# Chunk kernels of a state-space scan as products of the input tables with the output matrix

## Chip, cores and metric

The kernel runs on one core of a Trainium2 chip. The metric is the time of one execution in device microseconds (us); less is better. Before the change three runs took 1483.23, 1479.48 and 1482.27 us, a median of 1482.27.

## What is computed

Two transformer-like blocks over 528 positions (512 tokens and 16 meta tokens) of width 1024. The change concerns the first mixer of the first block, which has two branches: a state-space branch (S5, 32 groups of 16 channels with 64 complex states) and four mLSTM heads. Cut to the state-space branch, the reference is:

```python
dt = jnp.exp(log_dt)[:, None]
mag = jnp.exp(lam_re * dt)
ab_re, ab_im = mag * jnp.cos(lam_im * dt), mag * jnp.sin(lam_im * dt)   # a = exp(lambda dt)
bb = z * b                                                              # complex, z = (a - 1) / lambda
x[t] = a * x[t - 1] + bb @ u[t]                                         # associative scan over 528 positions
y = real(c @ x) + d * u
y_a = gelu(y); y_a = y_a * sigmoid(y_a @ w_glu)
```

Everything is float32. Large products are made of three passes (high by high, high by low, low by high part).

## The kernel before

The front of the program (`mixer`, from line 261) makes everything from eight input tiles. The 528 positions are cut into 66 chunks of 8. For each group the branch needs four things: what each chunk adds to the state (`inputs`), the recurrence from chunk to chunk (`recur`), what the state adds to the outputs of the next chunk (`back`, with the output table `CA`), and what the inputs of a chunk do to the outputs of the same chunk (`intra`, a Toeplitz matrix of the chunk kernel). The 32 groups go through in four sets of 8, m = 0 to 3.

- `prep(m)` (line 729) makes the input table `wt` on VectorE (`table`, lines 718 to 720: three operations over the whole table), turns it by eight transposes on TensorE (line 740), and ScalarE copies it to `ws` (line 742). `inputs(m)` multiplies `ws` with the chunk inputs `U` (line 752); ScalarE copies the result to `X` (line 756) and issues two transfers that put the swapped halves beside it (line 758).
- `recur` (line 800) is the recurrence on GpSimd: 64 steps of three operations each (lines 805 to 807), every step on all 32 groups, so that it starts after the last `X` transfer. Its result is read by the products of `X` with `CA` in `back` (line 821), which TensorE meets during the third head.
- `kernel(m)` (line 765) makes the output table `CA` (lines 718 to 720 again, now with 9 powers), multiplies `BB1` with it (line 776, eight products), copies the result to `kt` (line 778), adds the direct term `dm` (line 782), writes `kt` to a scratch buffer `kd` in DRAM behind 112 zeros (SyncE issues it, line 784), and reads it back through an overlapping pattern as the Toeplitz tile `tm` (ScalarE issues it, line 786). `intra(m)` multiplies `tm` with `U` (line 796).
- `Mlstm.proj(h)` makes the four projections of head h (q, k, v, output gate); each is 48 products (line 178) of a weight tile that `split_w` loads (SyncE, line 165) and splits into `wh` (ScalarE, line 167) and `wl` (VectorE, line 168).

Products of the branch share four PSUM buffers, `m`, with the attention core of the heads; the projections have two buffers, `d`. A list scheduler fixes the order on every engine when the program is built; `issue_after` and the order of calls steer it. Each engine runs its own list in order, and a transfer that ScalarE or SyncE issues stands in that list too: what comes behind it waits while it waits.

In time: the four input projections (u0 to u3) come first, then head 0 with `prep` and `inputs` between its projections, then head 1 with `kernel` and `intra` between them, then the cores of heads 0 to 3 beside the projections of heads 2 and 3 and the output side.

Of the kernel before, what the change touches and what calls it, by code (L numbers as in the profile page):

```python
# [9 lines left out]
F = mybir.dt.float32  # L10
# [12 lines left out]
G, NP, GH, NCH = 32, 64, 16, 66  # L23
# [237 lines left out]
def mixer(c):  # L261
    nc, tc, I = c.nc, c.tc, c.I
    V, A, P = nc.vector, nc.scalar, nc.gpsimd
    xh, xl = c.xh, c.xl
    with ExitStack() as ctx:
# [8 lines left out]
        def dense_ps():  # L274
            return pd.tile([128, 2, 512], F, name="d", tag="d")
# [8 lines left out]
        ssm = Ssm(c, hp, fs, misc, dr)  # L284
# [33 lines left out]
        def proj_full(idx, w=None):  # L318
            w = w or c.split_w(I["w1"][idx], 1024)
            ps = dense_ps()  # L320
            c.mm3([ps[:, 0, :264], ps[:, 1, :264]], w, 8,
                  lambda k, p: xh[:, k, 264 * p : 264 * p + 264], lambda k, p: xl[:, k, 264 * p : 264 * p + 264])
            return ps
# [16 lines left out]
        ml.gates()  # L340
        ssm.load()
        coeffs, first, root = ssm.coeffs(), ml.proj(0), c.root
        for m in range(4):
            with tc.high_priority():
                w = c.split_w(I["w1"][m], 1024) if m else w0
            ps = proj_full(m, w)
            u = fs2.tile([128, 8, NCH], F, name="u", tag="sa", bufs=2)
            for p in range(2):
                V.tensor_tensor(u[:, ::-1, 33 * p : 33 * p + 33].rearrange("p j c -> p c j"),
                                ps[:, p, :264].rearrange("p (c j) -> p c j", j=8),  # L350
                                rstd[:, 264 * p : 264 * p + 264].rearrange("p (c j) -> p c j", j=8), op=OP.mult)
            ssm.load_u(m, u)
            with tc.issue_after(root.ins) if m else ExitStack():
                if m < 2:
                    next(coeffs, None)
        for m in range(4):
            next(first, None)
            ssm.prep(m)
            if m:
                ssm.inputs(m - 1)  # L360
        ssm.inputs(3)
        ssm.recur()
        ssm.powers()
        ssm.pads()
        first = ml.proj(1)
        ssm.kernel(0)
        ssm.kernel(1)
        ml.rows(fs2)
        for m in range(4):
            next(first, None)  # L370
            dense = c.mm
            with tc.issue_after(ml.last.ins):
                if m < 2:
                    ssm.kernel(m + 2)
            with tc.issue_after(dense.ins):
                if m:
                    ssm.intra(m - 1)
                if m == 3:
                    ssm.intra(3)
        for _ in first:  # L380
            pass
        fctx.close()
# [79 lines left out]
        for m in range(8):  # L462
            w = c.split_w(I["wo1"][m], 1024)
            ps = dense_ps()
# [6 lines left out]
        for m in range(8):  # L471
# [3 lines left out]
            t = op.tile([128, 2, HF], F, name="pt", tag="pt", bufs=2)  # L475
# [104 lines left out]
class Ssm:  # L580


    def __init__(self, c, pool, front, misc, dram):
# [8 lines left out]
        self.AR = pool.tile([128, 2, 2, G], F, name="AR")  # L592
        self.U, self.ws, self.tm = {}, {}, {}

# [18 lines left out]
    def coeffs(self):  # L613
        c, nc, ss = self.c, self.c.nc, self.ss
        V, A = nc.vector, nc.scalar
        lr, li, sg = c.v("lam_re", 0, G), c.v("lam_im", 0, G), c.v("sgn")
        t = self.t32
        dt = c.exp_small(c.v("log_dt", 0, G), G)
        a = t("a")
# [14 lines left out]
        q = t("q")  # L634
# [25 lines left out]
        nr, den, zr, zi, m = t("nr"), t("den"), t("zr"), t("zi"), t("m")  # L660
# [20 lines left out]
        def bc(x):  # L681
            return x.unsqueeze(2).to_broadcast([128, G, GH])

        V.tensor_mul(self.BB1, B1, bc(zr))
        V.tensor_mul(m3, B2, bc(zis))
        V.tensor_sub(self.BB1, self.BB1, m3)
# [12 lines left out]

    def powers(self):  # L700
        V = self.c.nc.vector
        t = self.fs2.tile([128, 2, 9, G], F, name="cpow", tag="ws", bufs=2)
        self.prs, self.pin = t[:, 0], t[:, 1]
        for o, x, a in ((self.prs, self.pr, self.c.v("sgn")), (self.pin, self.pi, -1.0)):
            V.tensor_scalar_mul(o.rearrange("p e g -> p (e g)"), x.rearrange("p e g -> p (e g)"), a)

    def table(self, eng, out, tmp, x1, x2, p1, p2, gs, e0, ne):

# [13 lines left out]
    def load_u(self, m, u):  # L722
        nc = self.c.nc
        U = self.U[m] = self.hp.tile([128, 8, NCH], F, name="U", tag="qkv", bufs=11)
        ud = self.dr.tile([8, 128, NCH], F, name="ud", tag="ud")
        nc.scalar.dma_start(ud.rearrange("r p c -> p r c"), u)
        nc.scalar.dma_start(U.rearrange("p g c -> p (g c)"), ud.rearrange("r (h g) c -> (r h) (g c)", g=8))

    def prep(self, m):
        c, nc, ss, misc = self.c, self.c.nc, self.ss, self.misc  # L730
        V, A = nc.vector, nc.scalar
        gs = 8 * m
        wt = ss.tile([128, 8, 8, GH], F, name="wt", tag="t4", bufs=2)
        tmp = ss.tile([128, 8, 8, GH], F, name="tmp", tag="tt", bufs=1)
        self.table(V, wt, tmp, self.BB1, self.BB2, self.pr, self.pis, gs, 0, 8)
        ws = self.fs2.tile([128, 8, 128], F, name="ws", tag="ws", bufs=2)
        for q in range(2):
            ps = misc()
            for j in range(4):
                nc.tensor.transpose(ps[:, 128 * j : 128 * j + 128],  # L740
                                    wt[:, 4 * q + j].rearrange("p e h -> p (e h)"), c.idn)
            A.copy(ws[:, 4 * q : 4 * q + 4].rearrange("p g m -> p (g m)"), ps)
        self.ws[m] = ws

    def inputs(self, m):
        c, nc, misc = self.c, self.c.nc, self.misc
        A = nc.scalar
        gs, U, ws = 8 * m, self.U[m], self.ws[m]
        for q in range(2):
            ps = misc()  # L750
            for j in range(4):
                nc.tensor.matmul(ps[:, NCH * j : NCH * j + NCH], ws[:, 4 * q + j], U[:, 4 * q + j],
                                 start=True, stop=True)
# [5 lines left out]

    def ctable(self, m):  # L760
        tmp = self.ss.tile([128, 8, 9, GH], F, name="tmp", tag="t4", bufs=2)
        self.table(self.c.nc.vector, self.CA[:, 8 * m : 8 * m + 8], tmp, self.rc[:, 0], self.rc[:, 1], self.prs, self.pin,
                   8 * m, 0, 9)

    def kernel(self, m):
        c, nc, ss, misc = self.c, self.c.nc, self.ss, self.misc
        V, A, P = nc.vector, nc.scalar, nc.gpsimd
        gs = 8 * m
        U = self.U[m]
        ca = self.CA[:, gs : gs + 8]  # L770
        self.ctable(m)
        kt = self.fs2.tile([GH, 8, 128], F, name="kt", tag="kt", bufs=1)
        for q in range(2):
            ps = misc()
            for j in range(4):
                nc.tensor.matmul(ps[:GH, 128 * j : 128 * j + 128], self.BB1[:, gs + 4 * q + j],
                                 ca[:, 4 * q + j, 0:8].rearrange("p e h -> p (e h)"), start=True, stop=True)
            A.copy(kt[:, 4 * q : 4 * q + 4].rearrange("p g x -> p (g x)"), ps[:GH])
        dm = self.fs2.tile([GH, 8, GH], F, name="dm")
        V.tensor_mul(dm, c.idn[:GH, :GH].unsqueeze(1).to_broadcast([GH, 8, GH]),  # L780
                     c.v("d_t", gs, 8, GH).unsqueeze(2).to_broadcast([GH, 8, GH]))
        V.tensor_add(kt[:, :, :GH], kt[:, :, :GH], dm)
        kd = self.kd[m]
        nc.sync.dma_start(kd[:, :, 112:], kt)
        tm = self.tm[m] = self.fs2.tile([128, 8, 128], F, name="tm", tag="tm", bufs=3)
        nc.scalar.dma_start(tm, bass.AP(tensor=kd.tensor, offset=kd.offset,
                                        ap=[[16, 8], [1920, GH], [240, 8], [1, 128]]))

    def intra(self, m):

        nc, misc, A = self.c.nc, self.misc, self.c.nc.scalar
        gs, U, tm = 8 * m, self.U[m], self.tm.pop(m)
        for q in range(2):
# [790 lines left out]
@with_exitstack  # L1584
def build(ctx, tc, I, O, dbg=False, stages=3):
    c = Core(tc, ctx, I, O, dbg)
    with ExitStack() as c.fctx:
        c.pd = c.fctx.enter_context(tc.tile_pool(name="pd", bufs=2, space=PSUM))
        c.pm = c.fctx.enter_context(tc.tile_pool(name="pm", bufs=4, space=PSUM))
        rr = mixer(c)  # L1590
        if stages == 1:
            return
        ffn(c, rr)
        c.wpx = None
    if stages == 2:
        return
    with tc.tile_pool(name="apd", bufs=3, space=PSUM) as c.pd, tc.tile_pool(name="apo", bufs=1, space=PSUM) as c.po:
        attn(c)
        mlp(c)
# [15 lines left out]
```

## Time and profile before

| | |
|---|---|
| runs, median | 1482.27 us |
| profiled execution, its own time | 1480.72 us |
| its span (first to last instruction) | 1478.7 us |
| TensorE (PE) busy | 1436.9 us, 97% |
| VectorE (DVE) busy | 821.3 us, 56% |
| ScalarE (ACT) busy | 644.9 us, 44% |
| GpSimd (POOL) busy | 310.8 us, 21% |
| granted clock of TensorE, mean | 0.991 |

The span is cut by the profile into 40 equal slices; the digit of TensorE's granted clock is 9 (full speed) in all but the fourth, from 111 to 148 us, where it is 7. A row of the timeline gives the start and the length in us, engine, line, operation, what it writes and reads, how many, and in brackets how long the engine had been idle before and what ended that.

### The profile page before, as it was taken

What the parts mean: (1) busy time and instruction counts of PE and PEld (TensorE: products, weight loads), DVE (VectorE), ACT (ScalarE), POOL (GpSimd) and SP (SyncE); (2) the same over time, 40 slices, a digit from 0 to 9 for tenths busy, and PEclk for the clock granted to TensorE, in tenths of its full rate; (3) what the DMA queues carried; (4) which work ended last, traced back from release to release, by engine and by line L of the source; (5) the groups of instructions that cost most, each with busy time, mean ns of one, the idle gap of its engine ahead of it and who ended that gap; (6) DMA issues with size and microseconds to landing.
All of it is one profiled execution on the core that took longest, in us unless ns stands there. A gap on an engine that the chain in (4) does not pass through costs nothing.

```text
span 1478.7 us, 22651 instructions
## 1 busy us (share of the span) xinstructions
PE 1436.9 (97%) x9050; PEld 1295.2 (88%) x9050; DVE 821.3 (56%) x1463; ACT 644.9 (44%) x1032; POOL 310.8 (21%) x383
## 2 busy tenths in 40 slices
PE   7997999999999999999999899999998999999998
PEld 7996999999998998889988799999786788888887
DVE  8792654654437653256643668788776542244321
ACT  4453666733334433233332457677654531134310
POOL 0048860010124210001111513223444000000000
PEclk9997999999999999999999999999999999999999
DMA  5534123232522322332222133333222322322330
GB/s 171 145 90 89 58 71 89 66 107 81 175 90 71 100 85 85 109 107 87 79 88 92 44 116 114 110 99 101 67 73 93 104 100 100 100 90 96 107 121 29
DMA packets 62341, 140.33 MB, mean 95 GB/s; under 512 B 14742, under 2 KB 26902, under 8 KB 62236
## 3 DMA queue, kind: packets, MB, share of 16 engines
q1 hardware_dynamic: 44416, 126.72, 26.8%
q10 hardware_dynamic: 17820, 12.17, 3.6%
q8 instruction: 71, 1.16, 0.3%
q14 instruction: 34, 0.28, 0.1%
HBM read 128.83 MB, written 4.76 MB: 90 GB/s over the span
## 4 chain that ended last, share of the span: by engine, by line
PE 85%; DVE 7%; DMA 3%; issue 2%; ACT 1%; POOL 1%; ACTq 0%; DVEq 0%; POOLq 0%
PE d L178 17%; PE fm L178 16%; PE mp L178 12%; PE ad L178 9%; PE ad L1193 8%; PE fg L178 8%; PE ad L1404 3%; PE ao L178 3%; PE at L1314 1%; DMA kd<-kt 1%; DMA ud<-u 1%; PE m L999 1%; PE as L1289 1%; PE m L986 1%; PE as L1285 1%
## 5 line engine op out<-in xcount | busy, mean ns | idle before, releaser
L167 ACT CAST wh<-wr 128x1024 fp32r<-128x1024 f32 (+2 forms) x240 | 232.9, 972 | 534.0 <-PE fm L178 101.1
L168 DVE TENSOR_TENSOR wl<-wr,wh 128x1024 fp32r<-128x1024 f32 (+2 forms) x240 | 294.0, 1227 | 210.8 <-ACT wh L167 208.9
L178 PE MATMUL d<-xh,wl 128*128 128x258 f32 (+1 forms) x576 | 121.0, 290 | 1.7 <-DVE wl L168 1.7
L178 PE MATMUL d<-xh,wh 128*128 128x258 f32 (+1 forms) x576 | 121.3, 292 | 0.0
L178 PE MATMUL d<-xl,wh 128*128 128x258 f32 (+1 forms) x576 | 120.1, 289 | 0.0
L1193 PE MATMUL ad<-wh,xh 128*128 128x256 f32 x384 | 111.2, 293 | 2.5 <-ACT wh L167 1.3
L1193 PE MATMUL ad<-wh,xl 128*128 128x256 f32 x384 | 110.4, 289 | 1.4 <-DVE xl L570 1.2
L1193 PE MATMUL ad<-wl,xh 128*128 128x256 f32 x384 | 110.1, 289 | 0.5 <-DVE wl L168 0.4
L178 PEld LDWEIGHTS d<-xh,wl 128*128 128x128 f32 x576 | 91.4, 193 | 4.6 <-issue 2.3
L178 PEld LDWEIGHTS d<-xh,wh 128*128 128x128 f32 x576 | 91.4, 193 | 2.5 <-issue 1.0
L178 PEld LDWEIGHTS d<-xl,wh 128*128 128x128 f32 x576 | 91.7, 193 | 0.6 <-issue 0.4
L1116 POOL TENSOR_TENSOR gt<-gt,ga 128x512 f32<-128x512 f32 x22 | 31.5, 1434 | 267.5 <-ACT wh L167 202.9
L1193 PEld LDWEIGHTS ad<-wh,xh 128*128 128x128 f32 x384 | 74.0, 194 | 3.7 <-ACT xh L569 1.6
L1193 PEld LDWEIGHTS ad<-wh,xl 128*128 128x128 f32 x384 | 74.4, 194 | 2.6 <-DVE xl L570 2.2
L1193 PEld LDWEIGHTS ad<-wl,xh 128*128 128x128 f32 x384 | 74.2, 194 | 0.9 <-DVE wl L168 0.6
L178 PE MATMUL fg<-xh,wh 128*128 128x258 f32 x352 | 71.5, 284 | 1.9 <-ACT xh L569 1.9
L178 PE MATMUL fg<-xl,wh 128*128 128x258 f32 x352 | 71.3, 284 | 2.0 <-DVE xl L570 2.0
L533 POOL TENSOR_TENSOR nacc<-nacc,nsq 128x512 f32<-128x512 f32 (+1 forms) x37 | 52.7, 1425 | 91.9 <-ACT nsq L529 88.5
L178 PE MATMUL fg<-xh,wl 128*128 128x258 f32 x352 | 71.4, 284 | 0.0
L178 PE MATMUL fm<-xh,wh 128*128 128x512 f32 x176 | 70.1, 398 | 0.1
L178 PE MATMUL fm<-xl,wh 128*128 128x512 f32 x176 | 70.0, 398 | 0.0
L178 PE MATMUL fm<-xh,wl 128*128 128x512 f32 x176 | 69.7, 396 | 0.0
(459 smaller groups left out, 3633.1 us busy)
## 6 DMA issues: line engine op xcount, KB each, us to landing
wr<-in_wd_dram SPq DMA_DIRECT2D x48, 512.0 KB, 3.5
wr<-in_wgu_dram SPq DMA_DIRECT2D x44, 512.0 KB, 3.5
wr<-in_w_dram SPq DMA_DIRECT2D x36, 512.0 KB, 3.6
wr<-in_wup_dram SPq DMA_DIRECT2D x32, 512.0 KB, 3.5
wr<-in_wqkv_dram SPq DMA_DIRECT2D x24, 512.0 KB, 3.8
wr<-in_wo_dram SPq DMA_DIRECT2D x10, 512.0 KB, 4.7
wr<-in_wab_dram SPq DMA_DIRECT2D x16, 256.0 KB, 2.6
wr<-in_wd_dram SPq DMA_DIRECT2D x16, 192.0 KB, 2.3
```

The costliest lines, as they stand in the source:

```text
L167: nc.scalar.copy(hi[:, :n], raw[:, :n])
L168: (eng or nc.vector).tensor_sub(lo[:, :n], raw[:, :n], hi[:, :n].bitcast(F))
L178: self.mm = self.nc.tensor.matmul(o, a[:, k, :], x(k, p), start=first and k == order[0] and t == 0, stop=last and k == order[-1] and t == 2)
L533: self.eng.tensor_add(self.parts[0], self.parts[0], sq)
L986: nc.tensor.matmul(ps[:n, : b - a], k[:, s : s + n], q[:, t0 + a : t0 + b], start=True, stop=True)
L999: nc.tensor.matmul(o, Pt[:n, b : b + 128], Vt[:n, i, :129], start=i == 0, stop=i == j)
L1116: P.tensor_mul(t, t, a)
L1193: nc.tensor.matmul(o, x[:, k, 128 * tt : 128 * tt + 128], w[:, k4], start=k == 0 and i == 0 and tt % 2 == 0, stop=k == 7 and i == 2, skip_ ...
L1285: nc.tensor.matmul(ps[:, b:e], q, kh[:, :n], start=True, stop=False, skip_group_check=True)
L1289: nc.tensor.matmul(ps[:, b:e], q, kl[:, :n], start=False, stop=True, skip_group_check=True)
L1314: nc.tensor.transpose(pt[:, e : e + 128], p[:, off[i] + 128 * j : off[i] + 128 * j + 128], c.idn)
L1404: nc.tensor.matmul(ps, x[:, k], y[:, k, :S], start=i == 0 and t == 0, stop=i == kt - 1 and t == 2)
```

## The change

- The chunk kernel of a set is no longer a product with the output table `CA`. It is a product of the input table `wt`, which `prep` makes anyhow, with the output matrix `c` (line 767 of the changed kernel, eight products per set with an output of 128x16). For this the sign is multiplied into `c` once (line 678), and `powers` makes one table less.
- `kernel(m)` therefore moves into `prep(m)`, beside head 0, ahead of `recur`. Its tile `kt` is now 128 partitions by 8 groups by 16, one copy (line 769) instead of two. The write to `kd` is now 1024 pieces of 64 bytes, where it was 128 pieces of 512 bytes; both are 64 KB. `kt` has two buffers instead of one, `tm` four instead of three.
- The zeros in front of `kd` (`pads`) are written at the start of the program.
- The output tables are made by `ctable(m)` beside head 1, after the evictions of its projections; `intra(m)` stands after each of its projections.

```diff
+        ssm.pads()
         for m in range(4):
             next(first, None)
             ssm.prep(m)
@@
         ssm.powers()
-        ssm.pads()
         first = ml.proj(1)
-        ssm.kernel(0)
-        ssm.kernel(1)
         ml.rows(fs2)
         for m in range(4):
             next(first, None)
-            dense = c.mm
             with tc.issue_after(ml.last.ins):
-                if m < 2:
-                    ssm.kernel(m + 2)
-            with tc.issue_after(dense.ins):
-                if m:
-                    ssm.intra(m - 1)
-                if m == 3:
-                    ssm.intra(3)
+                ssm.ctable(m)
+            with tc.issue_after(c.mm.ins):
+                ssm.intra(m)
@@ coeffs
+        rc = self.rc[:, 0].rearrange("p g h -> p (g h)")
+        V.tensor_scalar_mul(rc, rc, sg)
@@ prep
         self.table(V, wt, tmp, self.BB1, self.BB2, self.pr, self.pis, gs, 0, 8)
+        self.kernel(m, wt)
@@ kernel
-        self.ctable(m)
-        kt = self.fs2.tile([GH, 8, 128], F, name="kt", tag="kt", bufs=1)
-        for q in range(2):
-            ps = misc()
-            for j in range(4):
-                nc.tensor.matmul(ps[:GH, 128 * j : 128 * j + 128], self.BB1[:, gs + 4 * q + j],
-                                 ca[:, 4 * q + j, 0:8].rearrange("p e h -> p (e h)"), start=True, stop=True)
-            A.copy(kt[:, 4 * q : 4 * q + 4].rearrange("p g x -> p (g x)"), ps[:GH])
+        kt = self.fs2.tile([128, 8, GH], F, name="kt", tag="kt", bufs=2)
+        ps = misc()
+        for j in range(8):
+            nc.tensor.matmul(ps[:, GH * j : GH * j + GH], wt[:, j].rearrange("p e h -> p (e h)"),
+                             self.rc[:, 0, gs + j], start=True, stop=True)
+        A.copy(kt.rearrange("p g h -> p (g h)"), ps[:, : 8 * GH])
@@
-        V.tensor_add(kt[:, :, :GH], kt[:, :, :GH], dm)
+        V.tensor_add(kt[:GH], kt[:GH], dm)
         kd = self.kd[m]
-        nc.sync.dma_start(kd[:, :, 112:], kt)
-        tm = self.tm[m] = self.fs2.tile([128, 8, 128], F, name="tm", tag="tm", bufs=3)
+        nc.sync.dma_start(bass.AP(tensor=kd.tensor, offset=kd.offset + 112,
+                                  ap=[[GH, 8], [1920, GH], [240, 8], [1, GH]]), kt)
+        tm = self.tm[m] = self.fs2.tile([128, 8, 128], F, name="tm", tag="tm", bufs=4)
```

**On ScalarE.** Before, beside head 1, the last three reads of the Toeplitz tile (`tm<-kd`, line 786) stand among the copies of the chunk kernel (`kt`) and of `intra` (`Yi`), long behind the transfers of `X`:

```order
L786 DMA tm<-kd 128x8x128
L778 COPY kt<-m 16x512 x2
L167 CAST wh<-wr 128x1024
L929 ACTIVATE k<-cy 128x528
L786 DMA tm<-kd 128x8x128
L778 COPY kt<-m 16x512 x2
L798 COPY Yi<-m 128x264 x3
L786 DMA tm<-kd 128x8x128
L798 COPY Yi<-m 128x264
```

Now, beside head 0, the first two of them (line 778 now) stand like this, with the copies to `X` of the first set and their transfers behind the second:

```order
L778 DMA tm<-kd 128x8x128
L921 ACT_TABLE_LOAD
L921 ACTIVATE q<-cy 128x528
L167 CAST wh<-wr 128x1024
L918 ACTIVATE cy<-cv,vec 128x528
L1029 ACT_TABLE_LOAD
L1029 ACTIVATE ls_e<-ls_e 4x528
L769 COPY kt<-m 128x128
L736 COPY ws<-m 128x512 x2
L750 COPY X<-m 128x264 x2
L778 DMA tm<-kd 128x8x128
L752 DMA X<-X 64x528 x2
```

All four reads have moved ahead of the last transfers of `X`, and each stands ahead of the next set's `kt` copy. The last read stands ahead of the transfers of sets 2 and 3, the ones `recur` starts after:

```order
L778 DMA tm<-kd 128x8x128
L752 DMA X<-X 64x528 x2
L750 COPY X<-m 128x264 x2
L899 COPY Ac<-m 128x16
L900 COPY Ac<-m 16x4
L902 ACT_TABLE_LOAD
L902 ACTIVATE em<-m 128x20
L752 DMA X<-X 64x528 x2
```

Before, no read of `kd` stood ahead of a transfer of `X`.

**On SyncE.** The writes of `kd` stand in the list of the weight loads. In the change, each of the four has a weight load directly ahead of it:

```order
L165 DMA wr<-in_w_dram 128x1024 x7
L775 DMA kd<-kt 8x128x16
L165 DMA wr<-in_w_dram 128x1024
L775 DMA kd<-kt 8x128x16
L165 DMA wr<-in_w_dram 128x1024
L775 DMA kd<-kt 8x128x16
L165 DMA wr<-in_w_dram 128x1024
L775 DMA kd<-kt 8x128x16
```

Behind the loads of the `ssm` tables, eleven weight loads stood ahead of the first two writes before; now seven stand ahead of the first.

## Rows read from the trace of the kernel before

**Rows 1.** Waits of TensorE, 30 to 150 us: total, times, longest.

```profile
PE m L796 <- ACT kt L778: 5.4, 1, 5.4
```

**Rows 2.** Timeline of TensorE, 100 to 150 us.

```profile
111.33 1.92 PE L776 MATMUL m<-CA,BB 128*16 128x128 f32 x16 [0.34 <-DVE CA L720]
...
121.75 3.68 PE L796 MATMUL m<-U,tm 128*128 128x66 f32 x16 [5.45 <-ACT kt L778]
...
129.05 0.40 PE L178 MATMUL d<-xh,wh 128*128 128x258 f32 x2
...
136.78 3.65 PE L796 MATMUL m<-U,tm 128*128 128x66 f32 x16 [4.39 <-DMA tm<-kd]
...
141.21 1.05 PE L958 MATMUL m<-idn,v 128*128 128x128 f32 x4
...
142.62 0.40 PE L178 MATMUL d<-xh,wh 128*128 128x264 f32 x2
```

**Rows 3.** Windows: length, busy us of the five engines, granted clock, DMA share, GB/s.

```profile
120.00:125.00 5.00, 3.25 (x15) 3.25 (x16) 0.28 (x1) 1.97 (x5) 4.22 (x11) 0.50 0.41 79
```

**Rows 4.** Timeline of ScalarE, 85 to 150 us (ACTq: its issued transfers).

```profile
120.44 0.58 ACTq L786 DMA_DIRECT2D tm<-kd  x1
121.12 1.05 ACT L778 COPY kt<-m 16x512 f32<-16x512 f32 x2 [6.18 <-DMA kd<-kt]
...
128.46 0.59 ACTq L786 DMA_DIRECT2D tm<-kd  x1
```

**Rows 5.** Timeline of GpSimd, 90 to 216 us: steps 1, 7 and 25, and the end.

```profile
92.80 1.25 POOL L805 TENSOR_TENSOR ra<-AR,X 128x128 f32<-128x128 f32 x1 [90.71 <-DMA X<-X]
...
115.90 0.52 POOL L805 TENSOR_TENSOR ra<-AR,X 128x128 f32<-128x128 f32 x1
...
142.67 0.53 POOL L805 TENSOR_TENSOR ra<-AR,X 128x128 f32<-128x128 f32 x1
...
213.52 0.35 POOL L807 TENSOR_TENSOR X<-X,rb 128x64 f32<-128x64 f32 x1
```

**Rows 6.** Timeline of TensorE, 212 to 224 us.

```profile
222.67 1.00 PE L821 MATMUL m<-X,CA 128*128 128x65 f32 x8
```

**Rows 7.** Timeline of VectorE, 54 to 86 us: eviction of head 0's q.

```profile
59.33 0.69 DVE L923 TENSOR_TENSOR cv<-d,rstd 128x528 f32<-128x528 f32 x1
```

**Rows 8.** Groups by line and shape, 0 to 330 us: count, busy us, mean ns.

```profile
L168 DVE TENSOR_TENSOR wl<-wr,wh 128x1024 fp32r<-128x1024 f32 x32 | 41.5, 1298 | 8.7 <-ACT wh L167 8.0
...
L167 ACT CAST wh<-wr 128x1024 fp32r<-128x1024 f32 x32 | 33.5, 1046 | 55.9 <-DMA ud<-u 21.2 <-PE d L178 17.4 <-issue 10.3
...
L929 ACT ACT_TABLE_LOAD x7 | 9.0, 1283 | 0.1
...
L926 ACT ACTIVATE cy<-cv,vec 128x528 f32<-128x528 f32 x8 | 6.6, 828 | 2.0 <-DVE cv L923 2.0
...
L718 DVE TENSOR_TENSOR tmp<-ssm_c,cpow 128x1152 f32<-128x1152 f32 x4 | 5.3, 1338 | 0.0
...
L756 ACT COPY X<-m 128x264 f32<-128x264 f32 x8 | 2.8, 378 | 1.2 <-PE m L752 1.2
...
L929 ACT ACTIVATE q<-cy 128x528 f32<-128x528 f32 x4 | 2.6, 645 | 1.7 <-DVE cy L928 1.6
...
L782 DVE TENSOR_TENSOR kt<-kt,dm 16x128 f32<-16x128 f32 x4 | 1.8, 458 | 6.0 <-ACT kt L778 6.0
...
L891 DVE TENSOR_TENSOR_SCAN B<-ls_e 4x528 f32<-4x528 f32 x1 | 1.2, 1245 | 0.0
```

**Rows 9.** Transfers of one tile, `kt`: time to landing.

```profile
DMA to landing us min/median/max: 2.5/5.2/6.8
```

**Rows 10.** Timeline of ScalarE, 30 to 90 us: write of `ud`, and the read that waits for it.

```profile
52.73 0.61 ACTq L726 DMA_DIRECT2D ud<-u  x1
...
58.18 0.33 ACTq L727 DMA_DIRECT2D U<-ud  x1
```

**Rows 11.** Transfers by line, 0 to 150 us: count, KB each, median us to landing.

```profile
X<-X ACTq DMA_DIRECT2D x8, 132.0 KB, 4.1
```

More of the change, by code (lines that the diff above doesn't have):

```diff
@@ L701, in powers @@
         V = self.c.nc.vector
[L702 to L705, printed above, removed]
+        self.pin = self.fs2.tile([128, 9, G], F, name="cpow", tag="ws", bufs=2)
+        V.tensor_scalar_mul(self.pin.rearrange("p e g -> p (e g)"), self.pi.rearrange("p e g -> p (e g)"), -1.0)
     def table(self, eng, out, tmp, x1, x2, p1, p2, gs, e0, ne):
@@ L761, in ctable, with kernel @@
         tmp = self.ss.tile([128, 8, 9, GH], F, name="tmp", tag="t4", bufs=2)
-        self.table(self.c.nc.vector, self.CA[:, 8 * m : 8 * m + 8], tmp, self.rc[:, 0], self.rc[:, 1], self.prs, self.pin,
+        self.table(self.c.nc.vector, self.CA[:, 8 * m : 8 * m + 8], tmp, self.rc[:, 0], self.rc[:, 1], self.pr, self.pin,
                    8 * m, 0, 9)
-    def kernel(self, m):
-        c, nc, ss, misc = self.c, self.c.nc, self.ss, self.misc
-        V, A, P = nc.vector, nc.scalar, nc.gpsimd
+    def kernel(self, m, wt):
+        c, nc, misc = self.c, self.c.nc, self.misc
+        V, A = nc.vector, nc.scalar
         gs = 8 * m
-        U = self.U[m]
-        ca = self.CA[:, gs : gs + 8]
-        self.ctable(m)
-        kt = self.fs2.tile([GH, 8, 128], F, name="kt", tag="kt", bufs=1)
-        for q in range(2):
-            ps = misc()
-            for j in range(4):
-                nc.tensor.matmul(ps[:GH, 128 * j : 128 * j + 128], self.BB1[:, gs + 4 * q + j],
-                                 ca[:, 4 * q + j, 0:8].rearrange("p e h -> p (e h)"), start=True, stop=True)
-            A.copy(kt[:, 4 * q : 4 * q + 4].rearrange("p g x -> p (g x)"), ps[:GH])
+        kt = self.fs2.tile([128, 8, GH], F, name="kt", tag="kt", bufs=2)
[4 more added lines that the diff above has]
+        A.copy(kt.rearrange("p g h -> p (g h)"), ps[:, : 8 * GH])
         dm = self.fs2.tile([GH, 8, GH], F, name="dm")
```

## Prediction

> **What bounds the kernel now.** The profile's first part puts TensorE at 97% of the span, so the question is which of its idle time the change removes and which it makes. I read the waits of TensorE first: around the scan the largest is for ScalarE's `kt` copy [rows 1]. The timeline shows it and a second one: before two of the four `intra` sets TensorE stands idle for 5.45 and 4.39 us [rows 2]. Behind each gap it runs slowly: sixteen passes with `tm` take 3.68 and 3.65 us there against 1.92 for sixteen passes of the chunk kernel, and the windows give a granted clock of 0.50 [rows 3], the lower of the two levels (1.2 GHz), after the engine had stood idle. The first gap comes from ScalarE's list: it stands 6.18 us before a `kt` copy, behind a read of `tm` that waits for the write of `kd` [rows 4]. A read in the list thus stops all that ScalarE has behind it.
>
> The second thing to read is the recurrence on GpSimd, which looks harmless because nobody waits for it: it starts at 92.80, when the last transfer of `X` lands, and ends at 213.52 + 0.35 = 213.87 [rows 5]. It has taken 121.1 us. TensorE meets its consumer, the product of `X` with `CA`, at 222.67 [rows 6]. The slack is 8.8 us. Whatever delays the start of the recurrence by more than that, or brings TensorE there earlier by more than that, makes GpSimd the bound.
>
> **The gain, if TensorE alone counted.** The four sets of `intra` get their `tm` long before they need it, so both gaps go: 9.84 us. So does the slow stretch behind each: 121.75 to 129.05 and 136.78 to 142.62 [rows 2], 13.1 us at half speed, of which half, 6.6 us, is lost. Together 16.4 us. The chunk kernels themselves are no gain: 32 products of two passes as before; the price of a pass is 1.92/16 = 0.12 us [rows 2], and the output is 16 columns instead of 128, whose cost I take as the same, since passes of 66 columns (3.65 us for 16 at half speed) cost as much as those of 128. That is 7.7 us of TensorE's time in all, moved from behind the recurrence's start to ahead of it.
>
> The small edits go together at nothing: one scaling of `c`, the memset and four issues of `pads` at the start, against one table of powers and one copy per set less. They can shift the start by perhaps 1 us either way.
>
> **What the move does to the recurrence's start.** In the new list of ScalarE each of the four reads of `tm` stands ahead of the next set's `kt` copy, and the last ahead of the last transfers of `X`. So four writes of `kd` and all ScalarE work between them become one chain that ends at the start of the recurrence. I add it up by means from the groups [rows 8], less 0.1 us for each hand-over on one engine:
>
> - Start: q of head 0 is evicted by 60.0 [rows 7], as before, since that eviction hangs on the earlier writes of `ud`. ScalarE's `cy` 0.83, `kt` copy about 0.3 (378 ns for 264 columns, fewer here), one convolution tap of VectorE and its `kt` addition 0.46: the first write is issued at about 62.2.
> - First read to second write: issue 0.6 [rows 4], table load 1.28, silu 0.65, cast 1.05, `cy` 0.83, table load 1.28, exponential 0.65, copy 0.3, addition 0.46: 7.1, less hand-overs 6.4 us.
> - Second read to third write: issue 0.6, two `X` issues 1.1, two table loads 2.56, two activations 1.3, cast 1.05, then on VectorE the weight split 1.30, the scan 1.25 and the addition 0.46: 9.6, less hand-overs 8.9 us.
> - Third read to fourth write: issue 0.6, one `X` issue 0.56, cast 1.05, table load 1.28, sigmoid 0.65, copy 0.3, addition 0.46: 4.9, less hand-overs 4.3 us.
> - Fourth read to the recurrence: issue 0.6, two `X` issues 1.1, two copies 0.7, one more issue 0.56, landing 4.1 [rows 11]: 7.0 us.
>
> With w for one write of `kd`, the recurrence starts at 62.2 + 6.4 + 8.9 + 4.3 + 7.0 + 4w = 88.8 + 4w.
>
> **The price of a write, bounded.** The writes before took 2.5 to 6.8 us with a median of 5.2 [rows 9], for 128 pieces each. Now each is 1024 pieces. The nearest row with as many pieces is the write of `ud` (1024 of 264 bytes): issued at 52.73, its reader released at 58.18, 5.45 us [rows 10]. Every new write has a weight load directly ahead of it in SyncE's list, and the three later ones have a read of `tm` in flight. I take 6.0, between 5.45 and the dearest write, and keep 2.5 and 6.8 as ends. No row shows a write in pieces of 64 bytes. The Trainium skill, DMA: Bandwidth & Descriptors, section Specifications, says that pieces under 512 B cost a read-modify-write; that speaks against this change, and by it w would lie at 6.8 or above. By that rule the sum below would be 18 us or more instead of 15.
>
> So the recurrence starts at 88.8 + 24 = 112.8, 20.0 us late.
>
> **Its length.** Its steps take three rates [rows 5]. The first 6, while VectorE makes tables, take 23.1 us (3.85 each); the next 18 take 26.8 (1.49), in the time when TensorE's gaps leave VectorE idle; the last 40 take 71.2 (1.78). After the change there is no such idle stretch, but TensorE's new wait makes one. From the start of the recurrence TensorE has about 21 us of head 1 left (three projections and four `intra` sets, less what passes while the last transfer lands), beside the tables on VectorE: 5.5 steps. From there to the product with `CA` it needs 222.67 - 141.21 = 81.5 us [rows 2, 6]: 46 steps at 1.78. The other 12.5 run at 1.49 while TensorE waits: 18.6 us. That is 121 us again.
>
> **The sum.** The recurrence ends at 112.8 + 121.1 = 233.9, and TensorE starts the product with `CA` at about 234.0 instead of 222.67: 11.3 us late, after standing idle for some 19 us. Behind so long a gap it runs at the lower clock first; I take the row of the 5.45 us gap, 7.3 us at half speed, 3.65 us lost [rows 2]. Nothing behind that place waits today (TensorE has no gap of note in the 100 us that follow), so nothing gives it back. In all 11.3 + 3.7 = 15.0 us. Against the profiled execution's own 1480.72 that is 1495.7; the median of the runs stands 1.55 higher, so I predict 1497.3 us. The 16.4 us of TensorE's gain come first and are eaten by the wait.
>
> **Rivals.**
>
> - *A, faster: GpSimd does not decide.* TensorE gains up to 16.4 us, 1466 us, or some 1470 if its own short waits for the `kt` copies stay. It decides from the point where the recurrence ends before 222.67 - 16.4 = 206.3. Even with the cheapest writes (4 x 2.5, start at 98.8) it would have to take 107 us, where it takes 121.1; GpSimd alone, at 1.49 a step, would do it in 95. It is possible only if the slow first steps are an accident. I give it 8%.
> - *B, no change: cheap writes.* With w at 2.5 the start is 98.8, the end 219.9; with 3.65 for the clock the kernel comes out 0.9 us later, 1483. Up to w = 3.3 it stays within 4.4 us. The first write before took 2.5, with nothing else in flight; here a load always is. 13%.
> - *C, dearer: longer steps and dear writes.* With w at 6.8 the end is 237.1, and the sum 18.2: 1500.5. If the tables also stop GpSimd, it adds up: before, about 9 us of table work ran inside the recurrence, now all twelve operations of 1.34 us [rows 8], 16 us; were every us of it lost, 7 us more, 1507. The Trainium skill, SBUF - State Buffer, section Who interferes with whom, says so: VectorE operations with both inputs in SBUF and GpSimd's reads exclude each other for a whole instruction. By that rule those 7 us count in full; the first six steps, at 3.85 instead of 1.49 beside tables, agree with it, and my 5.5 steps in 21 us already hold most of it. 19%.
> - *D:* the change does not do what it says (a `tm` read arrives late, and a gap of 4 us stays). The last read is issued 20 us before its use; it took 8.3 before. 2%, and it would be hidden in the wait anyway.
>
> **How the numbers follow.** The forecast (w from 3.4 to 6.5) has 58%, A 8, B 13, C 19, D 2. About 0.3% (4.4 us) is what a measurement of this kernel can tell from no change. Faster holds A, 0.08; within it B, 0.13; slower the rest, 0.79. The range leaves A out below and the last of C above: low 1480 (B with 1 us less from the small edits and a length 2 us shorter), high 1507 (C with all of its 7 us).
>
> **What would show it.** Right: no gaps before the `intra` sets; ScalarE idle four times for `kd<-kt`, some 4 to 6 us each; GpSimd's first step at 105 to 117 instead of 92.80; TensorE idle 10 to 25 us before the product with `CA`, released by GpSimd, and a lower granted clock there. Wrong: GpSimd's start below 100, or TensorE reaching that product without a wait; then the time falls below 1480. Wrong in size: a recurrence of under 112 or over 130 us.

## The result, and the profile after

The changed kernel takes 1497.36 us (median of four runs, 1495.33 to 1497.91) against 1482.75 (median of four, 1479.48 to 1484.18) for the kernel before: ratio 1.0099, 95% interval 1.0080 to 1.0119. That is 14.6 us slower. The profiled execution took 1497.57 us with a span of 1495.8.

The two gaps of TensorE before `intra` [rows 2] are gone. The last three sets run in 1.89 or 1.90 us each, where two took 3.68 and 3.65 at the lower clock. The waits of TensorE from 30 to 330 us (in total, times, longest) show what came instead:

```profile
PE m L813 <- POOL X L799: 21.9, 1, 21.9
PE m L746 <- ACT kt L769: 5.4, 2, 4.3
...
PE m L788 <- ACT X L750: 1.0, 1, 1.0
```

The timeline of TensorE (start, length, engine, line, operation; in brackets the idle time before it and what ended it):

```profile
72.65 1.98 PE L746 MATMUL m<-U,ws 128*128 128x66 f32 x8 [4.31 <-ACT kt L769]
...
114.35 1.89 PE L788 MATMUL m<-U,tm 128*128 128x66 f32 x16
...
122.01 1.89 PE L788 MATMUL m<-U,tm 128*128 128x66 f32 x16
...
186.91 3.70 PE L991 MATMUL m<-Vt,Pt 128*128 128x129 f32 x30
...
234.66 1.97 PE L813 MATMUL m<-X,CA 128*128 128x65 f32 x8 [21.92 <-POOL X L799]
...
236.38 0.78 PE L178 MATMUL d<-xh,wh 128*128 128x258 f32 x2
...
239.93 0.48 PE L178 MATMUL d<-xh,wl 128*128 128x258 f32 x2
240.25 0.41 PE L178 MATMUL d<-xh,wh 128*128 128x258 f32 x2
```

The product of `X` with `CA` starts at 234.66 instead of 222.67 [rows 6], 12.0 us late. Its first eight passes take 1.97 us instead of 1.00, and the slow stretch ends at about 239.9. Ahead of the wait TensorE is 10.1 us earlier than before (the product of `Pt` at 186.91), and behind the slow stretch it is 14.35 us later (the products at 240.25). The same rows in the kernel before:

```profile
197.00 3.71 PE L999 MATMUL m<-Vt,Pt 128*128 128x129 f32 x30
...
225.90 0.40 PE L178 MATMUL d<-xh,wh 128*128 128x258 f32 x2
```

The windows of the change show the granted clock in that stretch, and in the stretch behind the new wait for a `kt` copy at 72.65 (columns as in [rows 3]):

```profile
66.00:80.00 14.00, 9.69 (x57) 9.48 (x56) 8.78 (x13) 7.87 (x12) 0.00 (x0) 0.76 0.48 98
...
234.00:240.00 6.00, 5.34 (x27) 5.34 (x27) 0.43 (x1) 0.00 (x0) 0.52 (x2) 0.54 0.00 0
240.00:245.00 5.00, 5.00 (x44) 5.00 (x43) 0.84 (x3) 0.43 (x1) 0.00 (x0) 1.00 0.39 105
```

So some 5 us at half speed, 2.4 lost: 12.0 + 2.4 = 14.4, near the 14.6 us of the medians. The spans of the two profiled executions lie 17.1 us apart. The rest comes later, in further stretches at the lower clock: from 272 to 278 us the granted clock is 0.72 here, and 1.00 at the same products before.

GpSimd's timeline has the cause: its first step is 22.5 us later than before [rows 5], and the recurrence ends at 234.25 + 0.35 = 234.60 (the releaser in brackets is inferred; what the step needs is the last `X` transfer).

```profile
115.31 0.52 POOL L797 TENSOR_TENSOR ra<-AR,X 128x128 f32<-128x128 f32 x1 [113.22 <-DMA wr<-in_w_dram]
...
234.25 0.35 POOL L799 TENSOR_TENSOR X<-X,rb 128x64 f32<-128x64 f32 x1
```

The chain to that start stands in the transfers that SyncE and ScalarE issue. SyncE's writes of `kd`:

```profile
61.39 0.72 SPq L775 DMA_DIRECT2D kd<-kt  x1
...
72.93 0.61 SPq L775 DMA_DIRECT2D kd<-kt  x1
...
87.76 0.60 SPq L775 DMA_DIRECT2D kd<-kt  x1
...
97.15 0.61 SPq L775 DMA_DIRECT2D kd<-kt  x1
```

ScalarE's reads of `tm`, and what it issues and copies around the last:

```profile
65.69 1.18 ACTq L778 DMA_DIRECT2D tm<-kd  x1
...
76.90 0.61 ACTq L778 DMA_DIRECT2D tm<-kd  x1
...
91.89 0.64 ACTq L778 DMA_DIRECT2D tm<-kd  x1
...
97.67 0.72 ACT L750 COPY X<-m 128x264 f32<-128x264 f32 x2
103.93 0.65 ACTq L778 DMA_DIRECT2D tm<-kd  x1
104.67 2.34 ACTq L752 DMA_DIRECT2D X<-X  x2
...
108.25 0.61 ACTq L752 DMA_DIRECT2D X<-X  x1
```

Each read follows its write by 4.3, 4.0, 4.1 and 6.8 us. Before the last, ScalarE finishes its copies at 98.39 and stands until 103.93. The last transfer of `X` is issued at 108.25, and the recurrence starts 7.1 us after that.

### The profile page after: what moved, and what is told of

Read it like the earlier page. It is cut to its first block, busy times and chain, and to the rows that moved or that the text cites. A ratio compares the mean times of both kernels' runs of the same rounds, so it can differ in the third digit from the quotient of the medians.

```text
span 1495.8 us, 22640 instructions
## 1 busy us (share of the span) xinstructions
PE 1438.1 (96%) x9050; PEld 1298.3 (87%) x9050; DVE 821.9 (55%) x1463; ACT 640.8 (43%) x1028; POOL 311.3 (21%) x383
## 4 chain that ended last, share of the span: by engine, by line
PE 80%; POOL 8%; DVE 5%; DMA 3%; issue 2%; ACT 2%; ACTq 0%; DVEq 0%; POOLq 0%
PE fm L178 16%; PE d L178 13%; PE mp L178 12%; PE ad L178 9%; PE ad L1185 8%; PE fg L178 8%; PE ao L178 3%; PE ad L1396 3%; POOL ra L797 3%; POOL X L799 2%; POOL rb L798 2%; PE at L1306 1%; DMA ud<-u 1%; DMA kd<-kt 1%; PE as L1281 1%
```

## Experiments

The kernels were run beside the kernel before. "Start" is the first step of the recurrence, "wait" that of TensorE before the product of `X` with `CA`, both in the profiled execution; all in us. They were run in four groups, in which the kernel before has medians of 1482.75 (the change), 1483.92 (runs 1 to 4), 1481.39 (5 to 8) and 1483.85 (9 to 11). That is the same kernel, so medians of different groups can lie up to 2.5 us apart without a cause in the kernel; across groups the ratios are the fairer comparison.

| run | start | length | end | wait | median | ratio to before, 95% interval |
|---|---|---|---|---|---|---|
| before | 92.80 | 121.1 | 213.87 | 0 | | |
| the change | 115.31 | 119.3 | 234.60 | 21.9 | 1497.36 | 1.0099, 1.0080 to 1.0119 |
| 1 late reads | 96.96 | 123.8 | 220.73 | 10.1 | 1484.87 | 1.0009, 0.9998 to 1.0020 |
| 2 late reads, late `CA` | 97.68 | 125.2 | 222.91 | 0 | 1469.90 | 0.9902, 0.9887 to 0.9917 |
| 3 recurrence of 48 steps | 114.58 | 96.7 | 211.23 | 0 | 1472.79 | 0.9924, 0.9909 to 0.9938 |
| 4 wide writes | 111.72 | 119.2 | 230.94 | 21.5 | 1493.84 | 1.0066, 1.0049 to 1.0083 |
| 5 last read late | 106.65 | 124.2 | 230.88 | 19.1 | 1493.96 | 1.0085, 1.0067 to 1.0104 |
| 6 reads without wait | 106.64 | 122.8 | 229.49 | 19.9 | 1489.50 | 1.0050, 1.0031 to 1.0070 |
| 7 thin tables | 114.74 | 115.2 | 229.97 | 12.9 | 1493.00 | 1.0076, 1.0058 to 1.0094 |
| 8 reads on SyncE | 106.45 | 123.0 | 229.50 | 9.4 | 1477.46 | 0.9965, 0.9951 to 0.9980 |
| 9 wait without bytes | 104.65 | 124.7 | 229.31 | 11.5 | 1492.41 | 1.0051, 1.0036 to 1.0065 |
| 10 late `CA` alone | 115.36 | 124.2 | 239.54 | 9.4 | 1487.06 | 1.0020, 1.0006 to 1.0034 |
| 11 before, late `CA` | 93.03 | 120.8 | 213.83 | 0 | 1481.22 | 0.9990, 0.9971 to 1.0010 |

### Does GpSimd's recurrence decide? Runs 3, 10 and 11

**Run 3** cuts the recurrence from 64 steps to 48; the last 16 chunks get no state.

```diff
-        for k in range(1, NCH - 1):
+        for k in range(1, NCH - 1 - 16):
```

> The change, with the recurrence cut from 64 steps to 48 (the last 16 chunks get no state: part of the computation is left out). Theory: the recurrence starts at 115 as in the change and ends some 24 us sooner, at about 210, before TensorE's 212.7; the wait of 21.9 us and the slow clock behind it go: 1497.4 - 21.9 - 2.6 = 1473 (1470 to 1477). Rival (GpSimd only happens to be named; the tables or the order of the products hold TensorE): 1490 or more.

It took 1472.79 us, 24.6 less than the change (25.9 by the ratios): about the wait (21.9) and the slow clock behind it (2.4). The recurrence ends at 211.23, and the product with `CA` starts without a wait:

```profile
214.07 1.00 PE L813 MATMUL m<-X,CA 128*128 128x65 f32 x8
```

Tables, order and `kt` copies are the same, so it is the end of the recurrence that makes the change slower than the kernel before; without that wait it is faster.

**Run 10** moves the first product with `CA` one step later in TensorE's list, and **run 11** does the same to the kernel before.

```diff
-        weave([ml.core(2, ybh, ybl)], side, pipe[:2], limit=3, skip=1)
+        weave([ml.core(2, ybh, ybl)], side, pipe[:2], limit=3, skip=2)
```

> The change, with the first product of X with CA one step later in TensorE's list (skip=2) and the reads of tm where the change has them. Theory (only the recurrence's end counts): TensorE meets the product about 13 us of work later, at some 226, waits 8 to 10 us instead of 21.9, time 1497.4 - 13 = 1484 (1482 to 1487). Rival (the work moved ahead of the product is missed later): 1490 or more.

> The kernel before, with the same one step (skip=2). It waits for nothing there, so nothing should change: within 3 us of the kernel before, 1479 to 1486. If it came out 5 us or more faster, the gain of the run with late reads and the late product would be the step's own and not that of the removed gaps.

Run 10 came out at 1487.06, at the edge of what was expected. The wait fell to 9.4, but the recurrence ended 4.9 us later than in the change, from the same start. In the change its last 14 steps fall into TensorE's wait and take 1.4 us each; here TensorE works in part of that time, several steps take 2.3, and the 14 take 2.8 us more. The other 2.2 us are there before the 51st step (216.84 against 214.66); ten of the twelve table operations on VectorE fall into the recurrence here, nine in the change (see run 7). Run 11 shows no clear difference (0.3% faster to 0.1% slower): the step has no gain of its own.

### What delays its start? Runs 1, 5, 6 and 9

**Run 1** issues all reads of `tm` behind the last transfer of `X`.

```diff
         ssm.inputs(3)
+        with tc.issue_after(ssm.xd.ins):
+            for m in range(4):
+                ssm.toep(m)
         ssm.recur()
@@ kernel: the read of tm moved out
+    def toep(self, m):
+        nc, kd = self.c.nc, self.kd[m]
         tm = self.tm[m] = self.fs2.tile([128, 8, 128], F, name="tm", tag="tm", bufs=4)
         nc.scalar.dma_start(tm, bass.AP(tensor=kd.tensor, offset=kd.offset,
```

> The change, with one thing altered: the four reads of tm are issued behind the last transfer of X in ScalarE's list instead of between the kt copies; everything else keeps its order. Theory (the reads' waits for kd, standing in ScalarE's list, delay the recurrence): ScalarE no longer waits before its kt copies, GpSimd's first step starts at 92 to 97 instead of 115.3, the recurrence takes about 120 us and ends at 212 to 217; TensorE reaches the product with CA at 205 to 209 and still waits 5 to 10 us; time about 1476 (1470 to 1481). Rival 1 (the extra products, copies and additions beside head 0, not the reads, delay the X transfers): the start stays at 108 or later, time 1490 or more. Rival 2 (the bytes of kd and tm crowd the X transfers): the start comes only some 3 to 6 us earlier, time 1491 to 1495.

The start fell to 96.96, as expected, but the time only to 1484.87, a miss. The timeline of ScalarE:

```profile
94.37 0.61 ACTq L755 DMA_DIRECT2D X<-X  x1
95.02 1.17 ACTq L784 DMA_DIRECT2D tm<-kd  x1
...
96.23 10.97 ACTq L784 DMA_DIRECT2D tm<-kd  x3
```

Now the last `X` transfer needs 2.6 us from its issue (94.37 to 96.96), not 7.1. That the time did not follow has two reasons. The recurrence is 123.8 us long, 4.5 more than in the change: 2.2 us more before its 51st step, now that all twelve table operations fall into it, and 2.3 in the last 14 steps, of which fewer fall into a wait. And TensorE still loses time to the lower clock behind its wait, which is 10.1 us here. So the product with `CA` starts at 220.78, 1.9 us sooner than before the change, and the clock takes that back.

**Run 5** moves only the last read behind `X`.

> The change, with only the last of the four reads of tm moved behind the last transfer of X; all other instructions keep their order on every engine. Theory (a read ahead of X costs twice: its wait for kd, 5.5 us from 98.4 to 103.9 in the change, and its 512 KB, which stand ahead of the X transfers in ScalarE's queue, so that the last of these takes 7.1 us to land where it took 2.6 with all reads late): the recurrence starts 9 to 10 us sooner, at 105 to 107, time about 1488 (1485 to 1491). Rival (every read takes an equal share of the 18.4 us between the change and the run with all reads late): start at 110 to 111, time about 1493.

The start is 106.65: one read of four makes 8.7 of the 18.4 us, as expected. The time is 1493.96, a miss by 6: the recurrence is 4.9 us longer again, 4.0 of it before its 51st step, with all twelve table operations inside.

**Runs 6 and 9** take a read apart. Run 6 keeps the four reads at the change's places, from a buffer of zeros, so that they wait for no write. Run 9 puts there a read of 1 KB that waits for the same write, and the real reads behind `X`.

```diff
@@ run 6, toep
-        nc, kd = self.c.nc, self.kd[m]
+        nc, kd = self.c.nc, self.kz
@@ run 9
+    def touch(self, m):
+        s = self.fs2.tile([GH, GH], F, name="touch", tag="touch", bufs=4)
+        self.c.nc.scalar.dma_start(s, self.kd[m][:, 0, 112:128])
```

> The change, with the four reads of tm at the same places of ScalarE's list, but from a scratch buffer of zeros written at the start of the program (the chunk kernel is left out of the result; its writes stay). The waits go, the bytes stay ahead of X. Theory (waits and bytes both count): start at 100 to 103, between the 97.0 of the run with late reads and the 115.3 of the change; time 1486 to 1490. If only the waits count: start at 97 to 98, time 1484 to 1486. If the bytes do most of it: start at 106 or later, time 1490 or more.

> The counterpart of the run with reads but no wait: at the four places of the change's reads of tm, ScalarE issues a read of 1 KB of kd (into a tile that nobody uses) that waits for the same write; the real reads of tm stand behind the last transfer of X. The waits stay, the bytes ahead of X go. Theory (waits and bytes add up: 97.0 with neither, 106.6 with bytes alone, 115.3 with both, so 8.7 us for the waits): start at 104 to 108, time 1490 to 1494. If a write lands sooner when no 512 KB read is in flight: start at 100 to 104, time 1486 to 1490. If the waits count for nothing without the bytes: 97 to 99, 1485.

Run 6 starts its recurrence at 106.64, run 9 at 104.65, with times of 1489.50 and 1492.41. In run 6 the last issue of `X` on ScalarE's queue is far ahead of GpSimd's first step:

```profile
96.17 0.65 ACTq L793 DMA_DIRECT2D tm<-kz  x1
96.92 2.33 ACTq L764 DMA_DIRECT2D X<-X  x2
...
100.49 0.61 ACTq L764 DMA_DIRECT2D X<-X  x1
```

```profile
106.64 0.80 POOL L812 TENSOR_TENSOR ra<-AR,X 128x128 f32<-128x128 f32 x1 [104.55 <-DMA X<-X]
```

6.2 us. In run 9, with the read of 1 KB in its place, 2.7 us:

```profile
99.14 0.31 ACTq L792 DMA_DIRECT2D touch<-kd  x1
99.55 1.12 ACTq L764 DMA_DIRECT2D X<-X  x2
...
101.91 0.61 ACTq L764 DMA_DIRECT2D X<-X  x1
```

```profile
104.65 1.59 POOL L816 TENSOR_TENSOR ra<-AR,X 128x128 f32<-128x128 f32 x1 [102.57 <-DVE cv L934]
```

The first `kt` copy starts at 60.47 in run 1, 62.22 in run 6, 61.54 in run 9 and 60.23 in the change. Counted from there, the start comes after 36.5 us with neither, 44.4 with the bytes (7.9 more), 43.1 with the waits (6.6 more) and 55.1 with both (18.6 more). So the bytes ahead of `X` cost about as much as the waits; 4.1 us appear only where both are there. The writes account for most of that: from the four writes to the four reads it takes 15.7 us in run 9, and 19.2 in the change, where the 512 KB reads are in flight beside them.

### What does the write cost? Run 4

```diff
-        nc.sync.dma_start(bass.AP(tensor=kd.tensor, offset=kd.offset + 112,
-                                  ap=[[GH, 8], [1920, GH], [240, 8], [1, GH]]), kt)
+        nc.sync.dma_start(bass.AP(tensor=kd.tensor, offset=kd.offset + 112,
+                                  ap=[[240, 128], [1, 128]]), kt.rearrange("p g h -> p (g h)"))
```

> The change, with each write of kd as 128 pieces of 512 bytes instead of 1024 of 64; the same bytes land in other places of kd (the chunk kernel that is read back is permuted). Theory A (the number of pieces makes the price of a write, as the prediction's 6.0 us took it): the four waits of ScalarE for kd fall to some 2.5 us each, the recurrence starts near 105 to 109, time 1486 to 1490. Theory B (a write's price is latency and what is in the queues ahead of it, whatever its pieces): the waits stay within 1 us of the change's, the start at 113 to 116, time 1495 to 1499.

Neither theory: the start is 111.72 (3.6 us sooner) and the time 1493.84 (3.5 less). The transfers of `kt` in this run:

```profile
DMA to landing us min/median/max: 2.3/3.1/5.4
```

From write to read it takes 3.0, 2.3, 3.3 and 5.5 us, against 4.3, 4.0, 4.1 and 6.8 in the change: 5.1 us less in all, 1.3 per write. The start, counted from the first `kt` copy (61.44 here) as for runs 6 and 9, is 4.8 us sooner. The Trainium skill, DMA: Bandwidth & Descriptors, section Specifications, has pieces under 512 B pay for a read-modify-write. The sign agrees; the amount is about 1.3 us for a write of 64 KB. (The last read stands one `X` copy earlier in ScalarE's list here, so not every tenth belongs to the pieces.)

### What makes the recurrence long? Run 7

```diff
-        tmp = self.ss.tile([128, 8, 9, GH], F, name="tmp", tag="t4", bufs=2)
-        self.table(self.c.nc.vector, self.CA[:, 8 * m : 8 * m + 8], tmp, self.rc[:, 0], self.rc[:, 1], self.pr, self.pin,
-                   8 * m, 0, 9)
+        gs, shp = 8 * m, [128, 8, 9, GH]
+        self.c.nc.vector.tensor_tensor(self.CA[:, gs : gs + 8], self.rc[:, 0, gs : gs + 8].unsqueeze(2).to_broadcast(shp),
+                                       self.pr[:, 0:9, gs : gs + 8].rearrange("p e g -> p g e").unsqueeze(3).to_broadcast(shp),
+                                       op=OP.mult)
```

> The change, with one of the three operations of each output table (the other two are left out, so CA lacks its second term). Theory (table operations on VectorE beside the recurrence stretch its steps to some 3.5 us against 1.45): 8 operations of 1.34 us go, and with them 10.7 x (1 - 1.45/3.5) = 6.3 us of the recurrence's 119.3: length 112 to 114, time about 1491 (1489 to 1493). If GpSimd does nothing at all during such an operation: 10.7 us less, 1487. If the slow first steps have another cause (the wait of head 1's other VectorE work): length 118 to 120, time 1496 to 1498.

The length fell to 115.2, by 4.1 us. In the change only nine of the twelve table operations run inside the recurrence (the first three end before 115.31), in the run three. So six went where the expectation counted eight, of some 1.47 us each in the trace: 8.8 us of VectorE's time. The 4.1 us hide part of what they cost. The 25th step starts 47.99 us after the first here, and 53.85 us after it in the change. Its row in run 7, and in the change:

```profile
162.73 0.53 POOL L798 TENSOR_TENSOR ra<-AR,X 128x128 f32<-128x128 f32 x1
```

```profile
169.16 0.52 POOL L797 TENSOR_TENSOR ra<-AR,X 128x128 f32<-128x128 f32 x1
```

So GpSimd got back 5.9 us, two thirds of the 8.8. The last 14 steps give 1.8 of it away again, since TensorE's wait, in which a step takes 1.4 us, is 12.9 us instead of 21.9. The Trainium skill, SBUF - State Buffer, section Who interferes with whom, says that VectorE and GpSimd contend for ports that they share, as an exclusive lock, when a VectorE operation has two inputs in SBUF and GpSimd reads. That GpSimd is slowed agrees; that it loses the full length of such an operation does not show here.

### A kernel that beats both: runs 2 and 8

**Run 2** is run 1 with the product with `CA` one step later (the line of run 10).

> As the run before, and the first product of X with CA stands one step later in TensorE's list (skip=2 instead of 1). Theory (GpSimd's recurrence is what TensorE waits for, nothing else): TensorE meets the product at about 220, after the recurrence's end at 212 to 217, waits for nothing, stays at full clock; the gain of 16.4 us of the prediction's first sum stands: 1466 (1462 to 1470). Rival (something else is the bound, or the later product delays the output side): no better than the run before, 1474 or more.

1469.90 us, 0.98% less than before the change (0.83 to 1.13%). TensorE's list reaches the product after the recurrence's end at 222.91 and does not wait:

```profile
225.44 1.11 PE L819 MATMUL m<-X,CA 128*128 128x65 f32 x8
```

**Run 8** is run 2 with the reads given to SyncE, directly behind their writes.

```diff
-        nc.scalar.dma_start(tm, bass.AP(tensor=kd.tensor, offset=kd.offset,
+        nc.sync.dma_start(tm, bass.AP(tensor=kd.tensor, offset=kd.offset,
```

> The run with late reads and the late product with CA, with the reads of tm issued by SyncE directly behind the write they wait for, instead of by ScalarE behind X. Theory (ScalarE's list and queue are what must stay free; SyncE has no work in the 4 to 7 us that it waits): no wait of TensorE for tm and none of ScalarE for kd, the recurrence starts at 94 to 98, time about 1468 (1464 to 1470), as good as or a little better than the 1469.9 of that run. Rival (the 512 KB reads crowd the X transfers from any queue): start at 100 or later, the recurrence ends after 225, TensorE waits before the product with CA, time 1471 or more.

A miss, and the rival's case: 1477.46 us. SyncE reads the third set at 92.75:

```profile
92.75 0.59 SPq L784 DMA_DIRECT2D tm<-kd  x1
93.44 1.47 SPq L165 DMA_DIRECT2D wr<-in_w_dram  x1
95.01 0.60 SPq L778 DMA_DIRECT2D kd<-kt  x1
```

ScalarE issues the last two transfers of `X` beside that, 4.8 us apart (0.5 in run 1):

```profile
96.66 0.47 ACTq L755 DMA_DIRECT2D X<-X  x1
...
101.50 0.47 ACTq L755 DMA_DIRECT2D X<-X  x1
```

The recurrence starts at 106.45 and TensorE waits 9.4 us. The gap of 4.8 us is itself a wait: by the trace's semaphore marks, the second of the two transfers waits on the semaphore that the third read counts up, and that read lands at 101.48. The crowding shows in the three `X` transfers before it: issued from 94.55 to 96.66, they land 8.2 to 9.3 us later, where such transfers take 2.2 us (median of four) in run 2. The Trainium skill, DMA: Bandwidth & Descriptors, section Issuing engines are not separate DMA queues, says that transfers share the same 16 DMA engines whoever starts them. The run agrees: reads that SyncE issues slow the transfers that ScalarE issues. It doesn't separate the read from the weight load behind it, another 512 KB at 93.44, which SyncE's wait for the third write had held back (88.94 in run 2).

## Why the prediction was right, and which of its terms were not

- **The mechanism and the sum.** The recurrence becomes the bound, its consumer comes 12.0 us late (11.3 predicted), the slow clock costs 2.4 (3.7 predicted), together 14.4 in the profile and 14.6 by the medians (15.0 predicted). Run 3 shows the mechanism: without the wait the change is 11.1 us faster than the kernel before. That the sum came so close is partly luck: a start 2.5 us later than forecast, a length 1.8 us shorter and 1.3 us less for the clock nearly cancel.
- **The start of the recurrence** was 115.31 against 112.8, and here two terms missed in opposite ways. The four writes took 4.3 + 4.0 + 4.1 + 6.8 = 19.2 us, where 4w was 24. The work between them took 96.1 instead of 88.8, and 4.4 of these 7.3 us are in the last piece, from the fourth read to the recurrence: 11.4 instead of 7.0. The step that failed there is "landing 4.1", the median of the old `X` transfers [rows 11]: from the last issue to the first step it took 7.1, behind a 512 KB read. That is 3.0 of the 4.4; the other 1.4 are in the issues ahead of it, two of which took 2.34 us where 1.1 was put. The text priced the reads by their wait alone. Runs 6 and 9 show that their bytes cost about as much. ScalarE itself stood 4.2, 1.9, 4.5 and 5.5 us for the four writes; the second wait is shorter than the 4 to 6 us that were forecast as a sign.
- **The length** was 119.3 (121.1 predicted), made as the text put it: first six steps of 3.0 to 4.4 us beside tables, 1.4 us each at the end while TensorE waits. Run 10 shows the other side of that: with a wait of 9.4 us the last 14 steps take 22.7 us, with one of 21.9 they take 19.9.
- **TensorE's gain of 16.4 us** had not been reached where the wait came. At the second head's product of `Pt` it was 10.1 us ahead (197.00 before, 186.91 after). The prediction's own count of the steps, 112.8 + 21 + 81.5, brought TensorE to the product with `CA` at 215.3, only 7.4 us ahead, which doesn't fit the 16.4; it came there at 212.7. The text had the new waits for `kt` copies only in rival A; they were 4.31 and 1.07 us, and there is a slow stretch behind the first. All of it was hidden in the 21.9 us. With the wait removed, the gain is 11.1 us with the reads of the change (run 3) and 14.0 with late reads (run 2), by medians. Between the profiled executions of run 2 and of the kernel before it is 8.8, because the one was 2.1 us above its median and the other 3.2 below.
- **The rivals.** A needed a recurrence that doesn't bind; no run with all 64 steps was shorter than 115 us, even with two thirds of the table work gone (run 7). B needed w of 3.3 or less; the four writes took 4.0 to 6.8. C's tables cost about two thirds of their length (run 7).

## What to carry to other kernels

A chain that nobody waits for has a slack, and the slack is the first number to look up before work is moved in front of it: here a start 22.5 us late, against a slack of 8.8, turned a gain of 11 (run 3) into a loss of 15. A transfer that is moved ahead in an in-order list must be priced twice, by what it waits for and by the bytes that it puts in front of later transfers, and moving it to another engine's queue (run 8) freed ScalarE of the wait for `kd`, but not its transfers of the bytes. A chain that is moved in time also changes its length, by what runs beside it: here it grew by up to 5 us when it started sooner (runs 1 and 5). Where two engines' lists meet, shifting the meeting point by one step can be worth as much as the change itself (15.0 us between runs 1 and 2), and nothing where nobody waits (run 11).

## What the runs showed of the hardware that was not expected

- Four 512 KB reads (in pieces of 512 bytes) issued in a row held ScalarE: the last three issues took 10.97 us in run 1, and ScalarE's next instruction came 11.75 us after the one before. In the change, where such reads came 11.2 and 15.0 us behind the one before, issuing one took 0.6 us.
- From its issue, the last `X` transfer of 132 KB released GpSimd after 2.6 and 2.7 us with no large read ahead (runs 1 and 9), and after 6.2 and 7.1 with one (run 6 and the change). In run 5, where ScalarE's last large read was issued 9.1 us before it and SyncE's last weight load 5.0, it took 5.3.
